# Two heads to a unit in the sparse-attention stage of a hybrid decoder layer

## The chip, the core and the metric

The kernel runs on one core of a Trainium2 chip. The metric is the device time of one execution in microseconds (us), median of the runs. The core's engines are TensorE (PE; its weight loads are shown as PEld), VectorE (DVE), ScalarE (ACT), GpSimd (POOL) and SyncE (SP), whose queue issues all transfers of this kernel.

## What is computed

One decoder layer on x of 1024 tokens by 1024 in float32: RMS norm, a projection of all branches, forgetting attention (FoX, 8 heads), native sparse attention (NSA, 8 heads that share 2 groups of keys and values), a gated merge, an output projection, an MLP with squared ReLU, a last norm. The change is in the NSA branch:

```python
# 8 heads of 64, 4 to a key/value group; query blocks of 128
p_cmp = masked_softmax(q @ kc.T * SCALE + bias_c, cmp_end <= qpos)      # 63 compressed keys
o_cmp = p_cmp @ vc
sel   = top_k(imp, 16)                # of 16 blocks of 64 keys: all of them
o_slc = masked_softmax(q @ k_slc.T * SCALE + bias, pos <= qpos) @ v_slc # causal
o_win = masked_softmax(q @ k_win.T * SCALE + bias, 0 <= qpos - pos < 512) @ v_win
o     = g0 * o_cmp + g1 * o_slc + g2 * o_win
merged = sigmoid(g_a) * (o_fox @ w_br_fox) + sigmoid(g_b) * (o @ w_br_nsa)
```

Float32 products are made of rounded high parts and remainders (`float32r`): a score takes two matmuls, a value product two (the rounded probabilities and their remainders against values stored as [high | low]), a projection three.

## The kernel before

`attention` runs two stages, FoX and NSA. In each, a list of units is worked off by `attend`. A unit of NSA (`nsa_unit`) is one head `h` and one pair `g` of query blocks, `a = 2g` and `b = 2g + 1`, so 32 units. It has two lists of steps:

- `s1`: for both query blocks the scores against compressed and selected keys, then against window keys (`scores`: two matmuls into a PSUM bank of tag `S`, then a VectorE instruction, L817, that adds the bias and finds the least value), and for each of three parts a `softmax` (exponential on ScalarE, reciprocal on VectorE, scaling by gate and sum on GpSimd).
- `s2`, made by `pv`: the probabilities go in chunks of up to four 128x128 blocks through TensorE transposes into a PSUM bank (`turn`, L160), ScalarE rounds them (L856), VectorE makes the remainders (L857), and two chunks later the value products add into `acc` (L157). When the last has been issued, `finish` adds the low rows to the high ones (L865, L866) and stores 64 x 256 results to `on_d`; those of the last head stay in SBUF.

`acc` is half of the one bank `accs`: `psA` gives the two halves in turn. A product has 256 columns, the two query blocks of one head. Three cases are not full: key block `b` is seen by query block `b` alone, and there the left half of the operand is a zero tile (`make_diag`; four matmuls of 256 columns a unit); the oldest window block `a - 4` is seen by query block `a` alone (two matmuls of 128 columns); the compressed part takes one matmul in place of two.

`attend` interleaves `s1` of a unit with `s2` of the one before (`interleave`, `s1` ahead by `LEAD`), and spreads a list `feed` of other TensorE work among them: projections of later heads and of the second key/value group, gates, the FoX half of the merge (`branch_fox`). `due` says which feed steps must have run before a unit, `holds` which may not run before one. Between the end of a unit's scores and its `s2` at least `LAT` (2 us by the planner's costs) of other work is set. The order of pairs within a head is `gorder = (3, 0, 2, 1)`, for head 4 `gorder4 = (0, 3, 2, 1)`. Row tiles exist twice for small pairs (g < 2) and twice for large ones. Bias rows `ww` (one tile a head, four transfers, two buffers) are loaded at a head's first unit; the bias of the compressed part, `wcmp`, is loaded for all heads at the start. At the end of the list `load_on` brings stored results back, `LEAVE` (7 us) of feed is kept for after the last unit, and `merge` begins with the NSA half of the merge, `branch(..., wide=True)`, 16 groups of twelve 512-column matmuls, each with two loads of `msn` tiles.

Of the kernel before, what the change touches and what calls it, by code (L numbers as in the profile page):

```python
# [124 lines left out]
class Kernel:  # L125
# [733 lines left out]
    def finish(self, pa, dst, j, q0, name):  # L859

        nc = self.nc
        own = slice(64 * j, 64 * j + 64)
        oth = slice(64 - 64 * j, 128 - 64 * j)
        t = self.att.tile([P, 256], F32, tag="ot", bufs=3, name=f"ot{name}")
        nc.scalar.copy(t[own], pa[oth])  # L865
        nc.vector.tensor_add(t[own], pa[own], t[own])  # L866
        if dst is not None:
            nc.sync.dma_start(dst[:, q0:q0 + 256], t[own])
            return
        on, c = self.on[q0 // H], slice(q0 % H, q0 % H + 256)  # L870
        nc.scalar.copy(on[own, 3, c], t[own])
        nc.vector.tensor_sub(on[own, 7, c], t[own], on[own, 3, c].bitcast(F32))
# [10 lines left out]
    def pv(self, chunks, acc_name, done):  # L883
# [14 lines left out]
        def mats(c):  # L898
            if state["first"]:
                box["acc"] = self.psA("acc" + acc_name)  # L900
            us = chunks[c][2](box[c])
            acc = box["acc"]
            for x, (w, th, tl, n) in enumerate(us):
                end = c == nch - 1 and x == len(us) - 1
                if tl is not None:
                    self.mm(acc[:, 0:n], w, tl, start=state["first"], stop=False)
                    state["first"] = False
                self.mm(acc[:, 0:n], w, th, start=False, stop=end)
            if c == nch - 1:
                done(acc)  # L910
# [9 lines left out]
    def fox_unit(self, h, g, qf, kf, vf):  # L920
# [45 lines left out]
        s2 = self.pv(chunks, f"f{h}_{g}", lambda acc: self.finish(acc, dst, j, g * 256, f"f{h}_{g}"))  # L966
# [12 lines left out]
    def nsa_unit(self, h, g, qf, ksf, kwf, vf):  # L979
        nc = self.nc  # L980
        j, g_ = h % 2, h // 4
        rows, s1 = {}, []

        def load_bias():
            if g == self.order(h)[0]:
                self.ww = self.att.tile([P, 640], F32, tag="ww", bufs=2, name=f"ww{h}")
                for x in range(4):
                    nc.sync.dma_start(self.ww[32 * x:32 * x + 32],
                                      ap(self.w_d, h * 32 * 768 + 127 - 32 * x, [[767, 32], [1, 640]]))
            rows["ww"] = self.ww  # L990

        s1.append((0, load_bias))
        a, b = 2 * g, 2 * g + 1
        for x, i in enumerate((a, b)):
            n = P * (i + 1)
            nm = f"n{h}_{i}"
            gt = lambda br, i=i: self.gate[:, i, 3 * h + br:3 * h + br + 1]
            t0 = max(0, i - 4)
            nw = P * (i + 1 - t0)

            def dp(x=x, nm=nm):
                if ("p", x) not in rows:
                    rows["p", x] = self.row_tile(g, "p" + nm)
                return rows["p", x]

            def dw(x=x, nm=nm):
                if ("w", x) not in rows:
                    rows["w", x] = (self.att.tile([P, CPAD + 512], F32, tag="W0", bufs=2, name="w" + nm) if g < 2
                                    else self.att.tile([P, CPAD + 640], F32, tag="W1", bufs=2, name="w" + nm))
                return rows["w", x]  # L1010

            near = max(0, n - 2 * P)
            spans = [(0, CPAD, "c", lambda i=i: self.wcmp[:, h, 56 - 8 * i:56 - 8 * i + CPAD],
                      lambda dw=dw: dw()[:, 0:CPAD])]
            if near:
                spans.append((CPAD, CPAD + near, "s",
                              lambda near=near: self.farb[:, h:h + 1].to_broadcast([P, near]), dp))
            spans.append((CPAD + near, CPAD + n, "s", lambda n=n, near=near: rows["ww"][:, 640 - (n - near):640],
                          lambda dp=dp, near=near: dp()[:, near:]))

            def slc_done(m, x=x, n=n, nm=nm, gt=gt):
                self.softmax(rows["w", x][:, 0:CPAD], m["c"], nm + "c", gt(0))
                self.softmax(rows["p", x][:, 0:n], m["s"], nm + "s", gt(1))

            self.scores(s1, qf, ksf, i, 0, spans, nm, slc_done)
            self.scores(s1, qf, kwf, i, t0 * P,
                        [(0, nw, "w", lambda nw=nw: rows["ww"][:, 640 - nw:640], lambda dw=dw: dw()[:, CPAD:])],
                        nm + "w",
                        lambda m, x=x, nw=nw, nm=nm, gt=gt: self.softmax(rows["w", x][:, CPAD:CPAD + nw], m["w"],
                                                                         nm + "w", gt(2)))  # L1030
        sb = lambda x, t: rows["p", x][:, t * P:(t + 1) * P]

        def wb(x, t):
            t0 = max(0, a + x - 4)
            return rows["w", x][:, CPAD + (t - t0) * P:CPAD + (t - t0 + 1) * P]

        cb = lambda x: rows["w", x][:, 0:P]
        vs = lambda t: vf()[:, t, 0, :]
        vw = lambda t: vf()[:, t, 1, :]
        pairs = [(lambda t=t: vs(t), lambda t=t: [sb(0, t), sb(1, t)]) for t in range(0, a + 1)]  # L1040
        pairs += [(lambda t=t: vw(t), lambda t=t: [wb(0, t), wb(1, t)]) for t in range(max(0, a - 3), a + 1)]
        pairs += [(lambda: self.vcmp[:, g_, :], lambda: [cb(0), cb(1)])]
        single = a >= 4
        chunks = []

        def pt(nb):
            th, tl = self.pt_tile(f"n{h}_{g}")
            return (th[:, 0:nb], tl[:, 0:nb]), th, tl

        def dg():  # L1050
            dh, dl = self.diag[self.dn % len(self.diag)]
            self.dn += 1
            dv = lambda t: t.rearrange("p (a b) -> p a b", b=P)[:, 1::2, :]
            return (dv(dh), dv(dl)), dh, dl

        x = 0
        while x < len(pairs) or single:
            two = pairs[x:x + 2]
            x += len(two)
            one = len(two) < 2 and single  # L1060
            if one:
                single = False
            nb = len(two) * 256 + (P if one else 0)
            fold = slice(256 * len(two) - 256, 256 * len(two)) if x == len(pairs) and two else None

            def blocks(two=two, one=one):
                r = [y for t in two for y in t[1]()]
                return r + ([wb(0, a - 4)] if one else [])

            def uses(bx, two=two, one=one, fold=fold):  # L1070
                r = []
                for y, t in enumerate(two):
                    c = slice(256 * y, 256 * y + 256)
                    r.append((t[0](), bx[1][:, c], None if c == fold else bx[2][:, c], 256))
                if one:
                    c = slice(256 * len(two), 256 * len(two) + P)
                    r.append((vw(a - 4), bx[1][:, c], bx[2][:, c], P))
                return r

            chunks.append((blocks, lambda nb=nb: pt(nb), uses, fold))  # L1080
# [4 lines left out]
        dst = self.on_d[h * HD:(h + 1) * HD, :] if h < NH - 1 else None  # L1085
        s2 = self.pv(chunks, f"n{h}_{g}", lambda acc: self.finish(acc, dst, j, g * 256, f"n{h}_{g}"))
        return s1, s2
# [3 lines left out]
    gorder4 = (0, 3, 2, 1)  # L1091

    def order(self, h):

        return self.gorder4 if h == 4 else self.gorder
# [3 lines left out]
    def attend(self, units, feed, holds=(), calls={}):  # L1099
# [7 lines left out]
        start = [0.0]  # L1107
        for u in units:
            start.append(start[-1] + sum(c for c, _ in u[0]) + sum(c for c, _ in u[1]))
# [26 lines left out]
        def one():  # L1136
            self.owed -= cum[self.fed + 1] - cum[self.fed]
            self.fed += 1
            while len(trail) > 1 and trail[1][0] <= self.att_ns - self.SLACK:
                trail.pop(0)  # L1140
# [6 lines left out]
        def emit(steps):  # L1147
            for c, f in steps:
                with self.tc.high_priority(offset=self.PRIO):
                    f()  # L1150
                self.att_ns += c
                if c:
                    trail.append((self.att_ns, self.last.ins))
                self.owed += c * rate()
# [18 lines left out]
    LAT1 = 8000.0  # L1173
    LEAD = 1.5
# [3 lines left out]
    def attention(self):  # L1178
# [71 lines left out]
        due, holds2 = [0] * 8 + [len(f2.steps)] * 8, []  # L1250
# [10 lines left out]
        for g in self.gorder4:  # L1261
            due.append(late[g > 1])
# [743 lines left out]
```

## Time and profile before

| | |
|---|---|
| median of 3 runs | 1605.89 us (1604.8 to 1607.16) |
| the profiled execution | 1607.07 us, its span 1605.3 us |
| TensorE busy | 1581.5 us of the span, 8333 matmuls and transposes |
| VectorE, ScalarE, GpSimd busy | 1091.5, 864.1, 349.9 us |

NSA units run from about 369 us to 857 us of the span. A matmul's recorded duration covers its whole passage, which overlaps the next one's; what one adds to a run of them is read from start to start.

### The profile page before, as it was taken

To read this page: it belongs to the slowest core of one execution; us is meant where nothing else is said; L and a number is where in the kernel's file an instruction comes from. 1 tells how busy PE (TensorE), PEld (TensorE's weight loads), DVE (VectorE), ACT (ScalarE), POOL (GpSimd) and SP (SyncE) were. 2 spreads that over 40 slices of the span, in tenths; PEclk is the share of its full clock that TensorE was granted. 3 is DMA by queue.
4 is the path that set the end of the run, shared out by engine and by line. 5 is a ranking of instruction groups with operands and counts; after the bars stand their busy time and mean duration, and the time that the engine had idled before them with its cause. 6 is when DMAs were issued, how large, how long until landed. Compare 5 with 4: busy or idle time off the path is not lost. (4 is left out here: it accounts for less than half of the span.)

```text
span 1605.3 us, 23955 instructions
## 1 busy us (share of the span) xinstructions
PE 1581.5 (99%) x8333; PEld 1345.2 (84%) x8333; DVE 1091.5 (68%) x2366; ACT 864.1 (54%) x1648; POOL 349.9 (22%) x431
## 2 busy tenths in 40 slices
PE   8999999999999999999999999999999999999997
PEld 7888888888888888898888888888888888888886
DVE  7656667656665675576766569766655689777876
ACT  6655656545554665567653256655555644333334
POOL 1122222122332322336430000233333100000004
PEclk9999999999999999999999999999999999999999
DMA  6311212342222212114338652554444696545312
GB/s 188 75 45 49 63 47 57 107 117 53 73 55 68 60 37 73 58 60 142 126 121 288 221 171 92 176 172 151 160 150 155 202 331 220 160 144 170 106 53 105
DMA packets 165233, 196.71 MB, mean 123 GB/s; under 512 B 21288, under 2 KB 100968, under 8 KB 165104
## 3 DMA queue, kind: packets, MB, share of 16 engines
q1 hardware_dynamic: 165112, 195.18, 38.3%
q8 instruction: 66, 1.08, 0.3%
q14 instruction: 55, 0.45, 0.1%
HBM read 139.99 MB, written 55.15 MB: 122 GB/s over the span
## 5 line engine op out<-in xcount | busy, mean ns | idle before, releaser
L157 PE MATMUL oX<-to,so 128*128 128x512 f32 x672 | 154.6, 389 | 0.0
L157 PEld LDWEIGHTS oX<-to,so 128*128 128x128 f32 x672 | 126.1, 188 | 26.2
L1836 ACT CAST to<-w 128x1024 fp32r<-128x1024 f32 x48 | 48.3, 1051 | 144.0 <-PE accs L157 53.2
L857 DVE TENSOR_TENSOR PTn<-ptn,PTn 128x512 fp32r<-128x512 f32 (+2 forms) x136 | 81.9, 610 | 49.0 <-ACT PTn L856 48.5
L856 ACT CAST PTn<-ptn 128x512 fp32r<-128x512 f32 (+2 forms) x136 | 69.4, 523 | 52.3 <-PE ptn L160 43.4
L157 PE MATMUL fX<-ht,w1h 128*128 128x512 f32 x384 | 95.0, 389 | 0.6 <-DVE ht L1542 0.6
L157 PE MATMUL accs<-PTn,Vnv 128*128 128x256 f32 x480 | 91.7, 305 | 0.0
L1674 POOL TENSOR_TENSOR ss<-w 128x512 f32<-128x512 f32 x14 | 22.1, 1580 | 314.2 <-DMA w<-in_w_ff_dram 193.6
L1947 POOL TENSOR_TENSOR z<-x,gf 128x512 f32<-128x512 f32 x14 | 18.7, 1354 | 308.0 <-DVE x L1885 303.8
L157 PEld LDWEIGHTS fX<-ht,w1h 128*128 128x128 f32 x384 | 72.0, 188 | 16.0 <-DVE ht L1542 1.1
L833 POOL TENSOR_SCALAR pf<-pf,rdf 128x896 f32<-128x896 f32 (+3 forms) x64 | 47.6, 749 | 164.9 <-DVE rdf L832 158.9
L157 PE MATMUL g<-hTl,wh_g 128*128 128x512 f32 (+1 forms) x288 | 77.9, 390 | 1.5 <-DVE hTl L308 1.5
L157 PE MATMUL oZ<-to,so 128*128 128x512 f32 x336 | 77.6, 389 | 0.0
L1664 DVE TENSOR_TENSOR w1l<-w,w1h 128x1024 fp32r<-128x1024 f32 (+1 forms) x32 | 34.6, 1081 | 60.0 <-ACT w1h L1663 60.0
L157 PEld LDWEIGHTS accs<-PTn,Vnv 128*128 128x128 f32 x480 | 72.6, 189 | 2.7 <-DVE otn L866 0.4
L157 PE MATMUL g<-hTh,wh_g 128*128 128x512 f32 (+1 forms) x288 | 74.5, 387 | 0.0
L157 PEld LDWEIGHTS oZ<-to,so 128*128 128x128 f32 x336 | 63.1, 188 | 13.1
L157 PE MATMUL g<-hTh,wl_g 128*128 128x512 f32 x256 | 72.0, 399 | 0.0
L1837 DVE TENSOR_TENSOR so<-hr,so 128x1024 fp32r<-128x1024 f32 x56 | 68.3, 1240 | 1.8 <-ACT so L1836 1.8
L1836 ACT CAST so<-hr 128x1024 fp32r<-128x1024 f32 x56 | 56.8, 1051 | 21.0 <-DMA hr<-hid_d 21.0
L830 ACT ACTIVATE pf<-pf,mf 128x896 f32<-128x896 f32 (+3 forms) x64 | 49.7, 777 | 24.3 <-DVE mf L817 21.6
L1837 DVE TENSOR_TENSOR to<-w,to 128x1024 fp32r<-128x1024 f32 x48 | 56.8, 1223 | 7.7 <-ACT to L1836 7.7
(521 smaller groups left out, 4322.0 us busy)
## 6 DMA issues: line engine op xcount, KB each, us to landing
w<-in_w_ff_dram SPq DMA_DIRECT2D x62, 512.0 KB, 4.7
hr<-hid_d SPq DMA_DIRECT2D x56, 512.0 KB, 4.6
wr_wo<-in_w_out_dram SPq DMA_DIRECT2D x20, 512.0 KB, 5.0
x<-in_x_dram SPq DMA_DIRECT2D x16, 512.0 KB, 6.8
wr_g<-in_w_in_dram SPq DMA_DIRECT2D x16, 512.0 KB, 3.9
hid_d<-h22s SPq DMA_DIRECT2D x32, 256.0 KB, 2.1
hid_d<-s2s SPq DMA_DIRECT2D x32, 256.0 KB, 2.0
hid_d<-s3h SPq DMA_DIRECT2D x32, 256.0 KB, 2.3
```

What stands on the lines that cost most here:

```text
L157: self.last = self.nc.tensor.matmul(*a, **k)
L830: nc.scalar.activation(p, p, AF.Exp, bias=nm, scale=-1.0, accum_out=den)
L833: nc.gpsimd.tensor_scalar(p, p, r, 1.0 if gate is None else gate, op0=OP.mult, op1=OP.mult)
L856: nc.scalar.copy(th, src)
L857: nc.vector.tensor_sub(tl, src, th.bitcast(F32))
L1664: nc.vector.tensor_sub(lo, src, hi.bitcast(F32))
L1674: e.tensor_add(p[:, 4:8], b[:, 0:4], b[:, 4:8])
L1836: nc.scalar.copy(o[:, 0, s], src)
L1837: nc.vector.tensor_sub(o[:, 1, s], src, o[:, 0, s].bitcast(F32))
L1947: nc.gpsimd.tensor_mul(y[:, c], x[:, c], gf[:, c])
```

## The change

A unit is now a pair `p` of heads that share keys and values, and a pair `g` of query blocks: 16 units. The probabilities of a key block for two heads and two query blocks stand side by side, and a value product has 512 columns into the whole of `accs`. Key block `b` is multiplied for query block `b` of both heads alone, into a strided half of `accs`, with no zero tiles; the window's oldest block the same way for query block `a`. The order within a pair is (0, 3, 1, 2). Row tiles exist once for each place of a unit, in two sets (small, large). `wcmp` is loaded at a pair's first unit (eight transfers), as is `ww` (eight; three buffers). `finish` adds two heads and stores 128 x 256. Only the last two units' results stay in SBUF. The feed holds one gate less ahead of the second value projection and three gates in halves; `load_on` is cut into steps; the NSA half of the merge goes through the first half of the tokens for six blocks of features, then the second half, then the last two blocks, with its place on TensorE fixed against the last attention steps. The DMA scratch of the program goes from the default to 256 bytes a partition.

```diff
-    def finish(self, pa, dst, j, q0, name):
+    def finish(self, pa, js, dst, q0, name):
...
+        for n, j in enumerate(js):
+            own = slice(64 * j, 64 * j + 64)
+            oth = slice(64 - 64 * j, 128 - 64 * j)
+            c = slice(256 * n, 256 * n + 256)
+            nc.scalar.copy(t[own], pa[oth, c])
+            nc.vector.tensor_add(t[own], pa[own, c], t[own])
...
-                box["acc"] = self.psA("acc" + acc_name)
+                box["acc"] = self.accs if whole else self.psA("acc" + acc_name)
...
+                o = n(acc) if callable(n) else acc[:, 0:n]
...
-    def nsa_unit(self, h, g, qf, ksf, kwf, vf):
+    def nsa_unit(self, p, g, qf, ksf, kwf, vf):
...
+            if g == self.order(p)[0]:
+                self.wc = self.att.tile([P, 2, 120], F32, tag="wcmp", bufs=2, name=f"wcmp{p}")
+                for x in range(8):
+                    nc.sync.dma_start(self.wc[16 * x:16 * x + 16],
+                                      ap(self.y_d, p * 4096 + 7 - x, [[128, 16], [2048, 2], [1, 120]]))
+                self.ww = []
+                for j in range(2):
+                    w = self.att.tile([P, 640], F32, tag="ww", bufs=3, name=f"ww{2 * p + j}")
...
+        of = lambda x: (lambda acc: acc.rearrange("p (j x q) -> p j x q", j=2, x=2)[:, :, x])
+        two = lambda t: t.rearrange("p (j q) -> p j q", j=2)
...
-        chunks.append((lambda: [sb(1, b), wb(1, b)], dg,
-                       lambda bx: [(vs(b), bx[1][:, 0:256], bx[2][:, 0:256], 256),
-                                   (vw(b), bx[1][:, 256:512], bx[2][:, 256:512], 256)]))
+        for t in range(a + 1):
+            chunks.append((lambda t=t: [sb(j, x, t) for j, x in four], lambda: pt(H),
+                           lambda bx, t=t: [(vs(t), bx[1], bx[2], H)]))
+        for t in range(max(0, a - 3), a + 1):
+            chunks.append((lambda t=t: [wb(j, x, t) for j, x in four], lambda: pt(H),
+                           lambda bx, t=t: [(vw(t), bx[1], bx[2], H)]))
+        chunks.append((lambda: [cb(j, x) for j, x in four], lambda: pt(H),
+                       lambda bx: [(self.vcmp[:, g_, :], bx[1], None, H)], slice(0, H)))
+        if a >= 4:
+            chunks.append((lambda: [wb(j, 0, a - 4) for j in range(2)], lambda: pt(256),
+                           lambda bx: [(vw(a - 4), two(bx[1][:, 0:256]), two(bx[2][:, 0:256]), of(0))]))
+        chunks.append((lambda: [sb(0, 1, b), sb(1, 1, b), wb(0, 1, b), wb(1, 1, b)], lambda: pt(H),
+                       lambda bx: [(vs(b), two(bx[1][:, 0:256]), two(bx[2][:, 0:256]), of(1)),
+                                   (vw(b), two(bx[1][:, 256:H]), two(bx[2][:, 256:H]), of(1))]))
...
+    KEEP = (3, 1), (3, 2)
...
-    gorder4 = (0, 3, 2, 1)
+    norder = (0, 3, 1, 2)
...
-            self.make_diag(np_, 1, (0, 2))
...
+            order = [(f, half) for fs in (range(6), range(6, 8)) for half in (0, 1) for f in fs]
...
+                with (self.tc.issue_after(self.ends[-4 if x < 4 else -1]) if wide and x > 1 else nullcontext()):
+                    part_(i, f, fx, half, n, box, x)
...
-    nc = _bacc.Bacc("TRN2", target_bir_lowering=False, num_devices=1)
+    nc = _bacc.Bacc("TRN2", target_bir_lowering=False, num_devices=1, dynamic_dma_scratch_size=256)
```

## Rows read from the trace of the kernel before

**Rows 1.** The page: span, then busy us (share) and instructions.
```profile
span 1605.3 us, 23955 instructions
PE 1581.5 (99%) x8333; PEld 1345.2 (84%) x8333; DVE 1091.5 (68%) x2366; ACT 864.1 (54%) x1648; POOL 349.9 (22%) x431
```

**Rows 2.** Windows of the NSA stage: stretch, length, each engine's busy us, clock, DMA.
```profile
390.00:482.00 92.00, 92.00 (x542) 81.24 (x541) 55.55 (x204) 53.10 (x131) 28.91 (x46) 1.00 0.23 63
482.00:543.00 61.00, 61.00 (x358) 53.63 (x357) 35.05 (x135) 33.78 (x87) 19.62 (x32) 1.00 0.23 64
600.00:660.00 60.00, 59.08 (x333) 51.18 (x331) 32.48 (x91) 31.67 (x72) 15.05 (x24) 1.00 0.24 71
724.00:775.00 51.00, 49.60 (x306) 43.47 (x305) 35.65 (x136) 37.73 (x94) 33.55 (x40) 1.00 0.44 144
857.00:866.00 9.00, 7.78 (x35) 6.12 (x34) 2.74 (x6) 1.05 (x1) 0.00 (x0) 1.00 0.83 267
```

**Rows 3.** Waits of PE from 390 to 866: us in total, times, longest.
```profile
PE ptn L160 <- DVE PTn L857: 1.9, 2, 1.1
PE sn_4w L157 <- DVE mn L817: 1.6, 1, 1.6
PE brn L157 <- DVE msn L1435: 1.2, 1, 1.2
PE ptn L160 <- DVE rdn_1s L832: 0.6, 1, 0.6
```

**Rows 4.** Groups by form, PE, whole span: count, busy us, mean ns.
```profile
L157 PE MATMUL accs<-PTn,Vnv 128*128 128x256 f32 x448 | 86.6, 309 | 0.0
...
L160 PE MATMUL ptn<-idn,wn 128*128 128x128 f32 x304 | 59.8, 272 | 0.0
L160 PE MATMUL ptn<-idn,pn 128*128 128x128 f32 x288 | 52.4, 274 | 2.5 <-DVE PTn L857 1.9 <-DVE rdn_1s L832 0.6
...
L157 PE MATMUL accs<-diag,Vnv 128*128 128x256 f32 x128 | 20.9, 285 | 0.0
...
L157 PE MATMUL accs<-PTn,vcmp 128*128 128x256 f32 x32 | 9.4, 294 | 0.0
...
L157 PE MATMUL accs<-PTn,Vnv 128*128 128x128 f32 x32 | 5.4, 249 | 0.0
```

**Rows 5.** Timeline of PE, three places: start us, us, instructions.
```profile
403.98 0.34 PE L157 MATMUL accs<-PTn,Vnv 128*128 128x128 f32 x2
404.15 0.41 PE L160 MATMUL ptn<-idn,pn 128*128 128x128 f32 x2
...
413.86 0.64 PE L157 MATMUL accs<-PTn,Vnv 128*128 128x256 f32 x4
414.34 0.39 PE L157 MATMUL g<-hTl,wh_g 128*128 128x512 f32 x1
...
599.98 1.99 PE L157 MATMUL nk<-hTh,wl_nk 128*128 128x512 f32 x8
601.80 0.39 PE L157 MATMUL nk<-hTl,wh_nk 128*128 128x512 f32 x1
```

**Rows 6.** Groups by form, DVE, 385 to 862 us: count, busy us, mean ns.
```profile
L857 DVE TENSOR_TENSOR PTn<-ptn,PTn 128x512 fp32r<-128x512 f32 x104 | 70.9, 689 | 45.7 <-ACT PTn L856 45.4
```

**Rows 7.** The page's DMA queues: packets, MB, share.
```profile
q1 hardware_dynamic: 165112, 195.18, 38.3%
q8 instruction: 66, 1.08, 0.3%
q14 instruction: 55, 0.45, 0.1%
```

**Rows 8.** Tile `accs`, 745 to 750 us: ns min/median/max, first and last start.
```profile
L157 PE MATMUL accs<-diag,Vnv x4: 277/282/384, 745.5 to 746.0; 128*128 128x256 f32 x4
...
L157 PE MATMUL accs<-PTn,Vnv x4: 281/282/386, 749.1 to 749.5; 128*128 128x256 f32 x4
L865 ACT COPY otn<-accs x1: 365/365/365, 748.2 to 748.2; 64x256 f32<-64x256 f32 x1
L866 DVE TENSOR_TENSOR otn<-accs,otn x1: 427/427/427, 748.6 to 748.6; 64x256 f32<-64x256 f32 x1
...
  PEld accs L157: 0.4, 1
```

**Rows 9.** Timeline of SP: start us, us, transfers issued.
```profile
351.14 3.59 SPq L988 DMA_DIRECT2D ww<-w_d  x8
354.77 3.87 SPq L1320 DMA_DIRECT2D wcmp<-y_d  x8
...
420.03 1.72 SPq L988 DMA_DIRECT2D ww<-w_d  x4
```

**Rows 10.** DMA issues: count, KB each, median us to landing.
```profile
ww<-w_d SPq DMA_DIRECT2D x32, 80.0 KB, 2.0
```

**Rows 11.** Timelines of PE and DVE: a first score, the last result.
```profile
369.44 1.02 PE L157 MATMUL sn<-ks,Qnq 128*128 128x512 f32 x4
...
856.62 0.42 DVE L872 TENSOR_TENSOR on<-otn,on 64x256 fp32r<-64x256 f32 x1 [0.47 <-ACT on L871]
```

More of the change, by code (lines that the diff above doesn't have):

```diff
@@ L881, in row_tile, with pv @@
         return self.att.tile([P, T], F32, tag="P1", bufs=2, name=name)
-    def pv(self, chunks, acc_name, done):
+    def pv(self, chunks, acc_name, done, whole=False):
         nc = self.nc
@@ L977, in make_diag @@
             self.diag.append((t[:, 0], t[:, 1]))
-    def nsa_unit(self, h, g, qf, ksf, kwf, vf):
+    def nsa_unit(self, p, g, qf, ksf, kwf, vf):
         nc = self.nc
-        j, g_ = h % 2, h // 4
+        g_ = p // 2
         rows, s1 = {}, []
+        a, b = 2 * g, 2 * g + 1
         def load_bias():
[L985 to L990, printed above, removed]
-        s1.append((0, load_bias))
[L993 to L1033, printed above, removed]
@@ L1056, in nsa_unit @@
[L1056 to L1080, printed above, removed]
@@ L1087, in nsa_unit, with order @@
+        dst = None if (p, g) in self.KEEP else self.on_d[p * P:(p + 1) * P, :]
+        s2 = self.pv(chunks, f"n{p}_{g}", lambda acc: self.finish(acc, (0, 1), dst, g * 256, f"n{p}_{g}"), True)
         return s1, s2
+    KEEP = (3, 1), (3, 2)
     gorder = (3, 0, 2, 1)
-    gorder4 = (0, 3, 2, 1)
-    def order(self, h):
-        return self.gorder4 if h == 4 else self.gorder
+    norder = (0, 3, 1, 2)
+    def order(self, p):
+        return self.norder
     LAT = 2000.0
@@ L1107, in attend @@
         start = [0.0]
+        wt = [(id(e), self.WS) for u in units for e in u[0]] + [(id(e), self.WV) for u in units for e in u[1]]
+        wt = dict(wt)
         for u in units:
-            start.append(start[-1] + sum(c for c, _ in u[0]) + sum(c for c, _ in u[1]))
+            start.append(start[-1] + self.WS * sum(c for c, _ in u[0]) + self.WV * sum(c for c, _ in u[1]))
         marks = [(start[v], u[2]) for v, u in enumerate(units)] + [(start[-1], len(feed))]
@@ L1138, in one @@
             self.fed += 1
+            if self.STATIC:
+                with self.tc.issue_after(self.last.ins):
+                    feed[self.fed - 1][1]()
+                return
             while len(trail) > 1 and trail[1][0] <= self.att_ns - self.SLACK:
@@ L1147, in emit @@
         def emit(steps):
-            for c, f in steps:
-                with self.tc.high_priority(offset=self.PRIO):
+            for e in steps:
+                c, f = e
+                with self.tc.high_priority(offset=self.PRIO), (
+                        self.tc.issue_after(self.last.ins) if self.STATIC else nullcontext()):
                     f()
+                c *= wt[id(e)]
                 self.att_ns += c
@@ L1153, in emit @@
                     trail.append((self.att_ns, self.last.ins))
+                    self.ends = self.ends[-3:] + [self.last.ins]
                 self.owed += c * rate()
@@ L1173 @@
     LAT1 = 8000.0
+    ends = []
+    STATIC = False
+    WS, WV = 1.0, 1.0
     LEAD = 1.5
@@ L1340 @@
     LEAVE = 7000.0
-    ON2 = 24
-    ON3 = 31
+    ON = 9, 17, 25
+    ON3 = 16
     FST = 6
@@ new lines, in branch, with part, part_ @@
+        ns = [self.wadd([(None, wa[:, f2 * 256:f2 * 256 + 256].rearrange("(k p) c -> p k c", p=P))],
+                        f"br{name}{f2}", shape=(4, 256)) for f2 in range(4)]
+        order = [(f, half) for f in range(8) for half in range(2)]
+        if wide:
+            order = [(f, half) for fs in (range(6), range(6, 8)) for half in (0, 1) for f in fs]
+        for x, (f, half) in enumerate(order):
+            n, fx, box = ns[f // 2], f % 2, {}
+            def part(i, f=f, fx=fx, half=half, n=n, box=box, x=x):
+                with (self.tc.issue_after(self.ends[-4 if x < 4 else -1]) if wide and x > 1 else nullcontext()):
+                    part_(i, f, fx, half, n, box, x)
+            def part_(i, f, fx, half, n, box, x):
+                hi, lo = self.wget(n)
+                if i == 0:
+                    box["sg"] = stage(f, half)
+                    psf = self.psS if wide and x % 5 > 1 else self.psP
+                    box["ps"] = psf(f"br{name}{f}{half}")
+                o = of()[half]
+                mm = [(w, k + d) for ks in ((0, 1, 2), (3,)) for w, d in ((lo, 0), (hi, 4), (hi, 0))
+                      for k in ks]
+                for m in range(6 * i, 6 * i + 6):
+                    w, k = mm[m]
+                    self.mm(box["ps"], w[:, k % 4, fx * P:(fx + 1) * P], o[:, k],
+                                     start=m == 0, stop=m == 11)
+                if i == 1:
+                    done(f, half, box["ps"], box["sg"])
+            for i in range(2):
+                st.add(6 * MM, lambda i=i, part=part: part(i), n)
```

165 lines of the change are left out of this document (85 added, 80 removed).

## The prediction

> **What bounds the kernel now.** I read the page's engine line first: TensorE is busy 1581.5 us of a span of 1605.3 us, the next engine, VectorE, 68% [rows 1]. A busy matmul row need not mean TensorE at its peak, so the second view is the windows of the NSA stage, read for stretches that fall short: from 390 to 543 us TensorE is busy without a gap and at the full granted clock of 1.00 (2.4 GHz), later stretches lack 0.9 to 1.4 us each, while VectorE stands at about 60% [rows 2]. The third view, TensorE's waits from 390 to 866 us, gives the size of everything that is not TensorE work: 1.9 + 1.6 + 1.2 + 0.6 = 5.3 us in five waits [rows 3]. So the stage lasts as long as TensorE's own list of instructions takes from start to start. A change is worth what it takes off that list, less or plus what it does to 5.3 us of waits. Work saved on other engines counts for nothing directly.
>
> **Value products: what is removed.** The counts before are 448 products of 256 columns on key blocks, 128 on the half-zero operands, 32 on the compressed part, and 32 of 128 columns on the oldest window block [rows 4]. After, by the diff: two heads share a product, so 448 + 32 become 240 of 512 columns; a unit's four products on block `b` serve two heads, so 128 become 64 of 256 columns; the 32 of 128 become 16 of 256. That is 640 matmuls before, 320 after.
>
> The recorded mean of about 300 ns is the whole passage of one matmul and no price. The price is start to start: four products of 256 columns from 413.86 to 414.34 us are 0.120 us each (0.1175 to 0.1225 with the rounding of both ends); eight matmuls of 512 columns from 599.98 to 601.80 us are 0.2275 us each; two of 128 columns take 0.17 us together [rows 5]. I take the low reading of the 256-column price, since a small gap could stand in the place read:
>
> - before: 608 x 0.1175 + 16 x 0.17 = 71.4 + 2.7 = 74.1 us
> - after: 240 x 0.2275 + 80 x 0.1175 = 54.6 + 9.4 = 64.0 us
> - difference: 10.1 us.
>
> Bounds: at 0.120 us it is 75.7 - 64.2 = 11.5 us. If only columns counted, at the 512-column rate of 0.2275/512 = 0.444 ns a column, 159,744 columns become 143,360, and 7.3 us are saved. Of the 10.1 us, the dropped zero columns (64 x 0.1175) make 7.5, the rest is the fixed few nanoseconds of 320 matmuls.
>
> These two prices can be weighed against the Trainium skill ("TensorE: Matmul & The Clock Gate", section "Back-to-back issue gap"), which gives an isolated full-clock gap of N/2.4 + 2.5 ns, 109 ns at 256 columns and 216 ns at 512. Both rows here are 5 to 10% above it; by the page's prices the saving would be an estimated 7.7 us, near my lower bound.
>
> **What stays.** Scores keep their pieces and number. The transposes stay 304 + 288 [rows 4], since every block of probabilities is still turned once. By the code, chunks fall from 184 to 152, so ScalarE and VectorE evict fewer, fuller banks; a full remainder on VectorE takes 689 ns [rows 6], and neither engine sets the end of this stage [rows 2]. That goes at nothing, hidden behind TensorE; if the cover were gone it would still be a gain. The zero tile's four GpSimd instructions go, at nothing. The smaller DMA scratch touches no transfer of this kernel as far as the queues show: all packets but 121 instruction fetches are on the hardware queue [rows 7]; cost nothing, its room goes to the larger row tiles. Moving a gate and splitting one more in halves leaves the same matmuls.
>
> **What is added: one accumulator.** The first product of a unit now waits until `finish` of the unit before has read the whole bank. In the trace that wait already shows: at one boundary the last product starts at 746.0 us, ScalarE's copy comes late at 748.2, VectorE's sum ends at 749.0, and the next unit's first product starts at 749.1, after a wait of 0.4 us on the weight load [rows 8]. Two heads add one sum of about 0.43 us behind the first, the second copy running beside it. TensorE normally has two groups of transposes and scores to do before it needs the bank. Floor: no wait, 0. Ceiling: every one of 15 boundaries as late as this one with the second sum on top, 15 x 0.83 = 12.5 us. I take 0.6 us: near the floor, since TensorE's waits in the whole stage name `finish` nowhere [rows 3].
>
> **What is added: loads at a pair's start.** Eight loads of `wcmp` and eight of `ww` per pair, where a head had four. Issue costs 0.43 to 0.48 us each (8 in 3.59, 8 in 3.87 us), landing 2.0 us [rows 9, 10], so 7.5 us of SP's queue and about 9.5 us until the last has landed. Most of it can be issued as early as now: the loads for head 2 go out at 420.03 us [rows 9], long before that head. Only the second head's `ww` must wait, with three buffers, until the first head of the running pair has had its last scores, half a unit's scores ahead. From the first score at 369 us to the last result at 857 us [rows 11] a pair unit lasts (857 - 369)/16 = 30 us on average, so that half is some 8 to 13 us ahead, and four loads need 4 x 0.45 + 2.0 = 3.8 us. Behind a waiting load on SP stand weight loads of the feed, which run two tiles ahead, and stores that nobody awaits. Cost nothing from below (no gain is possible), 9.5 us at each of three pair starts from above; I take nothing.
>
> **What is moved.** The order small, large, small, large keeps two units of one size from following each other; before, head 4's order set 1 next to 0 and 3 next to 2, and the wait of 1.6 us on the scores of block 4 lies there. Against it, the second group's keys must still be written between units 7 and 8, so that wait may return. Waits at unit starts (`ptn` on PTn and on `rdn_1s`, 2.5 us [rows 3]) can come 16 times instead of 32, each with twice the product work of the unit before to cover it: I take 1.2 us off. The merge's wait of 1.2 us comes from the loads of `msn`, whose room is freed by the end of the stage; this end is later relative to the loads (a large unit is last), and half the loads lie ahead as before: left as it is, bounds 0 and 3 us.
>
> **Sum.** -10.1 + 0.6 - 1.2 = -10.7 us. The profiled execution took 1607.07 us, its span 1605.3; the median of the runs is 1605.89. So the changed span should be about 1594.6, and the median 1605.9 - 10.7 = 1595.2 us.
>
> **Rivals.**
>
> - *Columns only, waits as before.* The saving is 7.3 us and the waits come to the same 5.3 us or up to 2 us more: 1598.6 to 1600.6 us. For it: transposes stand between products over most of the stage, so the fixed cost of a product may be hidden in part.
> - *Waits vanish too.* 11.5 us and all 5.3 us of waits: 1589.1 us. Against it: the merge's loads and the keys of the second group remain.
> - *The bank is the bound.* A wait at each boundary, 5 to 12.5 us in all: 1600 to 1607 us. Against it: a single 0.4 us in 31 boundaries as shown.
> - *Strided outputs.* The 80 products on single query blocks write two runs of 128 columns apart. No row before has such an output. If one cost twice its price, 80 x 0.1175 = 9.4 us return and the time is 1604.6 us, no change. The Trainium skill ("PSUM — Partial Sum Buffer", section "Specifications (TRN2)") says that any non-contiguous access pattern slows matmuls significantly; no run here shows it.
> - *Slower: pair loads come late.* If the waiting `ww` load holds SP's queue, then VectorE's first bias sums of the second head, and soon TensorE with three score banks full, stand for up to 9.5 us at three pair starts: 1595.2 + 28.5 = 1623.7 us. It decides from 3.6 us a pair on (10.7/3), and is slower than before beyond the measurement from 4.7 us. Against it: the lead of 8 to 13 us.
>
> **How the numbers follow.** Chances: the forecast, 1592 to 1598 us, 0.57; columns only 0.15; waits vanish 0.08; the bank 0.09; strided outputs 0.05; pair loads 0.06. The forecast and the first two rivals hold 0.80, so the range reaches from 1589 to 1602 us, which also takes in the mild half of the bank's case. About 0.2% (3.2 us) is what a measurement of this kernel can tell from no change: the first three cases and half of the bank's are faster, strided outputs and the rest of the bank's the same, late loads slower: 0.86, 0.08, 0.06.
>
> **What would show it.** TensorE's count falls by 320 to 8013 and its busy time by about 10 us; the runs of 512-column value products read 0.2275 us from start to start, those with strided outputs 0.12; the NSA stage ends some 10 us earlier and everything behind it keeps its length; TensorE's waits in the stage stay at 3 to 6 us. Wrong would be: a wait of `accs` weight loads on `otn` at most boundaries, a wait of `sn` scores on L817 behind `ww` at three places about a fourth of the stage apart, a strided product of 0.2 us or more, or a gap of several us where the merge begins.

## The result, and the profile after

The changed kernel takes 1591.7 us (median of 4 runs, 1591.63 to 1591.98), the kernel before 1605.78 us (4 runs, 1604.8 to 1607.16). The ratio is 0.9912, with an interval of 0.9895 to 0.9929: 14.1 us less, where 10.7 were forecast. The direction and the range held; the size is off by 3.4 us, and even the mild end of the interval (0.0071 x 1605.8 = 11.4 us) lies above the forecast. The time is just outside the band of 1592 to 1598 us that the forecast gave itself, and nearer to the rival in which the waits vanish too (1589.1 us) than to the forecast's 1595.2. The same kernel was run twice more, on two chips, each time beside the kernel before: 1592.21 and 1591.68 us, ratios 0.9909 and 0.9908. So the miss is no accident of one run.

The page after: span, then busy us, share and instructions of each engine, and the queue that carries the data.

```profile
span 1590.0 us, 23189 instructions
PE 1569.0 (99%) x8013; PEld 1320.0 (83%) x8013; DVE 1087.5 (68%) x2316; ACT 856.8 (54%) x1598; POOL 348.5 (22%) x427
...
q1 hardware_dynamic: 165400, 195.18, 38.3%
```

TensorE has 320 instructions less, as counted ahead, and 12.5 us less busy time, where about 10 were expected; it is still the only engine near its span; its queue of data carries the same 195.18 MB as before [rows 1, 7]. Where the 15.3 us of span went is read from three marks: the first `nq` matmul (the NSA stage's start), the first `wo` matmul (the merge's end) and the end. TensorE's timeline after, at the first two (start us, us, instructions):

```profile
337.70 2.11 PE L157 MATMUL nq<-hTh,wl_nq 128*128 128x512 f32 x8
...
873.84 0.62 PE L157 MATMUL wo<-wh_wo,ml 128*128 128x512 f32 x2
```

and before:

```profile
338.10 1.65 PE L157 MATMUL nq<-hTh,wl_nq 128*128 128x512 f32 x6
...
888.63 0.61 PE L157 MATMUL wo<-wh_wo,ml 128*128 128x512 f32 x2
```

Between the marks lie 550.5 us before and 536.1 after: 14.4 us of the 15.3. Ahead of them 0.4 us are gone and behind them 0.5 (716.7 to 716.2), where nothing was changed. How much such a stretch moves by itself is seen from the other runs of equal kernels below: 549.5 us for the kernel before with nothing but the smaller scratch, 536.4 and 536.4 for the two repeats of the changed one. So the stage gave 13.1 to 14.4 us.

TensorE's waits from 380 to 862 us of the changed kernel (us in total, times, longest):

```profile
PE accs L157 <- DVE PTn L847: 1.2, 2, 0.7
PE accs L157 <- DVE PTn L857: 1.0, 2, 0.5
```

These two lines answer to [rows 3]. 5.3 us in five waits became 2.2 us in four. None of the old places is left: not the scores of block 4 behind L817, not the first transposes behind L857 or L832, not the merge behind `msn`. What is left is of another kind: a value product (`accs`) waits for VectorE's eviction of its chunk. In the two waits for L847 it is the compressed chunk near the end of a unit's list; of the two for L857 one stands at a unit's first product (751.85 us), one among the window chunks of the last unit (831.56 us). And no line names `otn`: no wait for the single accumulator shows.

The groups by form on TensorE (count, busy us, mean ns, idle before):

```profile
L157 PE MATMUL accs<-PTn,Vnv 128*128 128x512 f32 x224 | 79.0, 433 | 1.0 <-DVE PTn L857 1.0
...
L160 PE MATMUL ptn<-idn,wn 128*128 128x128 f32 x304 | 51.9, 272 | 0.0
...
L160 PE MATMUL ptn<-idn,pn 128*128 128x128 f32 x288 | 48.1, 272 | 0.0
...
L157 PE MATMUL accs<-PTn,Vnv 128*128 128x256 f32 x80 | 13.5, 283 | 0.0
...
L157 PE MATMUL accs<-PTn,vcmp 128*128 128x512 f32 x16 | 7.0, 439 | 1.2 <-DVE PTn L847 1.2
```

240 products of 512 columns and 80 of 256, and as many transposes as in [rows 4]. Their prices stand in the timeline, start to start:

```profile
790.64 1.09 PE L157 MATMUL accs<-PTn,Vnv 128*128 128x512 f32 x4
791.57 0.60 PE L160 MATMUL ptn<-idn,wn 128*128 128x128 f32 x4
...
840.70 0.64 PE L157 MATMUL accs<-PTn,Vnv 128*128 128x256 f32 x4
841.17 0.86 PE L157 MATMUL brn<-on,wl_brn 128*128 128x512 f32 x3
```

Four products of 512 columns take 0.93 us, 0.2325 us each (0.2275 was forecast). Four of 256 columns with strided outputs take 0.47 us, 0.1175 us each: the price of plain ones [rows 5]. Over all of them the median spacing is 0.236 us for 512 columns and 0.118 us for 256, and 0.120 us for the 448 plain ones before.

A product beside a transpose takes longer to the next start than one beside a product, and the transpose behind it less, so the two are added up: all products and transposes of the stage, from each start to the next, without the idle time before an instruction. By the records of the traces this is 88.6 + 45.1 = 133.7 us before and 75.0 + 48.6 = 123.6 us after, 10.1 us less. The kernel before with the smaller scratch gives 133.7, the two repeats 123.6 each.

### The profile page after: what moved, and what is told of

Its sections match the earlier page's. It is cut to its first block, busy times and chain, and to the rows that moved or that the text cites. A ratio compares the mean times of both kernels' runs of the same rounds, so it can differ in the third digit from the quotient of the medians.

```text
span 1590.0 us, 23189 instructions
## 1 busy us (share of the span) xinstructions
PE 1569.0 (99%) x8013; PEld 1320.0 (83%) x8013; DVE 1087.5 (68%) x2316; ACT 856.8 (54%) x1598; POOL 348.5 (22%) x427
## 3 DMA queue, kind: packets, MB, share of 16 engines
q1 hardware_dynamic: 165400, 195.18, 38.3%
## 5 line engine op out<-in xcount | busy, mean ns | idle before, releaser
L857 DVE TENSOR_TENSOR PTn<-ptn,PTn 128x512 fp32r<-128x512 f32 (+1 forms) x136 | 91.2, 672 | 64.9 <-ACT PTn L856 63.9
L856 ACT CAST PTn<-ptn 128x512 fp32r<-128x512 f32 (+1 forms) x136 | 76.6, 570 | 72.2 <-PE ptn L160 61.1
L157 PE MATMUL accs<-PTn,Vnv 128*128 128x512 f32 (+1 forms) x304 | 92.6, 393 | 1.0 <-DVE PTn L857 1.0
L157 PEld LDWEIGHTS oZ<-to,so 128*128 128x128 f32 x336 | 63.1, 188 | 13.1
L830 ACT ACTIVATE pn<-pn,mn 128x128 f32<-128x128 f32 (+3 forms) x64 | 49.6, 776 | 18.6 <-DVE mn L817 16.3
```

The lines of the kernel that those rows point to most:

```text
L157: self.last = self.nc.tensor.matmul(*a, **k)
L830: nc.scalar.activation(p, p, AF.Exp, bias=nm, scale=-1.0, accum_out=den)
L856: nc.scalar.copy(th, src)
L857: nc.vector.tensor_sub(tl, src, th.bitcast(F32))
```

## The experiments

The stretch "stage" is always from the first `nq` to the first `wo` matmul of the run's profiled execution; 536.1 to 536.4 us for the changed kernel, with a mean of 536.3 in its three profiles, and 2.2 to 2.5 us of waits, with a mean of 2.4.

### The zero columns put back

The unit's last chunk multiplies key block `b` for the other query block too, by a tile of zeros: 64 more products of 256 columns. This has the columns of the kernel before (143,360 + 64 x 256 = 159,744) in 256 fewer matmuls.

```diff
-                       lambda bx: [(vs(b), two(bx[1][:, 0:256]), two(bx[2][:, 0:256]), of(1)),
-                                   (vw(b), two(bx[1][:, 256:H]), two(bx[2][:, 256:H]), of(1))]))
+                       lambda bx: [(x, y, z, of(q)) for x, c in ((vs(b), 0), (vw(b), 256)) for y, z, q in
+                                   ((two(bx[1][:, c:c + 256]), two(bx[2][:, c:c + 256]), 1),
+                                    (two(self.zz), two(self.zz), 0))]))
...
+            self.zz = np_.tile([P, 256], FR, tag="zz", bufs=1, name="zz")
...
```

> The changed kernel with the zero columns back: each unit also multiplies block b against a zero tile for query block a, 64 more products of 256 columns (strided output); the result is the same. Theory (the stage lasts as long as TensorE's list): 64 x 0.1175 = 7.5 us more, 1599.2 us. Rival (the stage is by now paced by waits on ScalarE and VectorE, and the work saved was only part of it): less than 3 us more, 1592 to 1594.5 us.

Measured: 1599.54 us, ratio 0.9961 (0.9949 to 0.9974), span 1597.6. The stage took 543.7 us (337.8 to 881.5), 7.4 more than the changed kernel's; 64 x 0.1175 = 7.5 were forecast. The waits of TensorE in its stage:

```profile
PE accs L157 <- DVE PTn L857: 1.0, 2, 0.6
PE accs L157 <- DVE PTn L847: 0.7, 1, 0.7
PE brf L157 <- DVE msf L1417: 0.3, 1, 0.3
```

2.0 us, as little as in the changed kernel, so the zero columns cost their full price. This run also parts the rest, though less sharply: with the same columns as before, the stage is 5.8 to 6.8 us shorter (549.5 and 550.5 against 543.7). 2.4 to 3.3 us of this are waits (4.4 and 5.3 against 2.0), and 3.4 to 3.5 us are left. If all of that came from the 256 fewer matmuls, it would be 13 ns for each. But products and transposes, summed as above, take 132.15 us here against 133.7, 1.6 us less or 6 ns for each; the gates' matmuls, whose number no edit touched, read 156.7 us against 158.5 in the same sum. So fewer matmuls at the same columns gave something between 1.6 and 3.5 us, and where the rest belongs stays open.

### The order, the merge's place, FoX

The order within a pair starts with a large unit and ends with a small one:

```diff
-    norder = (0, 3, 1, 2)
+    norder = (3, 0, 2, 1)
```

> The changed kernel with the pairs in the order (3, 0, 2, 1), large units first and small last, still large and small in turn. Theory (product work made the gain, order is worth the waits only): TensorE's waits in the stage grow from 2.2 to at most 5 us, 1592 to 1595 us. Rival (the order and the end of the stage made the third of the gain that the product sum did not hold): 3.6 us or more, 1595.3 us or above.

Measured: 1596.98 us, 0.9942 (0.993 to 0.9955), span 1595.3; the stage 541.3 us, 5.0 more. TensorE's waits in it:

```profile
PE accs L157 <- DVE PTn L857: 1.5, 2, 1.3
PE ptn L160 <- DVE PTn L857: 1.4, 2, 0.8
PE ptn L160 <- POOL pn L833: 0.9, 1, 0.9
PE sn_4w L157 <- DVE mn_1w L817: 0.5, 1, 0.5
PE accs L157 <- DVE PTn L847: 0.5, 1, 0.5
```

4.8 us, as the theory had it at most, but the time is the rival's: 5.3 us above the changed kernel's. The waits are 2.4 us more than there, and transposes wait again. The other 2.6 us are in no line of this view. Gaps of less than 0.15 us, which it leaves out, are 0.45 us more. And each stop costs more than its gap: a matmul with no successor behind it is recorded to the end of its passage (0.40 us for a 512-column product), where with one behind it the next starts after 0.236 us. There are 16 stops here, short ones counted, against 6; by the median spacing of each form this comes to an estimated 2.6 against 1.1 us; the trace models the ends of matmuls, so it is no more than an estimate. The last 0.7 us stay open.

The merge goes through its blocks as before, without a fixed place:

```diff
-            order = [(f, half) for fs in (range(6), range(6, 8)) for half in (0, 1) for f in fs]
+            pass
...
-                with (self.tc.issue_after(self.ends[-4 if x < 4 else -1]) if wide and x > 1 else nullcontext()):
+                with (self.tc.issue_after(self.ends[-4 if x < 4 else -1]) if False else nullcontext()):
```

> The changed kernel with the NSA half of the merge in the old order (both halves of the tokens for each block of features, no place fixed against the last attention steps). Theory (the forecast left this step as it is, 0): the wait at the start of the merge comes back as before, 1.2 us, 1592.9 us. Rival (nothing: the wait vanished because the loads come earlier for other reasons): 1591.7 us within 0.5 us. A third way: with a large unit last the loads come later than before, 3 us or more.

Measured: 1595.62 us, 0.9935 (0.9922 to 0.9947), span 1593.9; the stage 539.9 us, 3.6 more. The timeline of TensorE where the stage's last unit ends (in brackets the idle time before, and what ended it):

```profile
845.87 0.74 PE L157 MATMUL accs<-PTn,Vnv 128*128 128x256 f32 x4 [1.17 <-DVE PTn L857]
848.81 1.62 PE L157 MATMUL brn<-on,wl_brn 128*128 128x512 f32 x4 [2.21 <-ACT on L874]
850.23 3.17 PE L157 MATMUL brn<-on,wh_brn 128*128 128x512 f32 x8
853.24 0.84 PE L157 MATMUL brn<-on,wl_brn 128*128 128x512 f32 x3
```

and its windows (stretch, length, busy us of PE, PEld, DVE, ACT, POOL, granted clock, DMA):

```profile
843.00:849.00 6.00, 2.63 (x16) 2.00 (x15) 2.50 (x6) 1.72 (x4) 0.00 (x0) 1.00 0.01 3
849.00:853.00 4.00, 4.00 (x11) 3.16 (x11) 2.58 (x5) 0.82 (x1) 0.00 (x0) 0.57 0.66 174
853.00:858.00 5.00, 5.00 (x24) 4.13 (x22) 4.78 (x8) 1.37 (x3) 0.00 (x0) 1.00 0.89 301
```

After the last product everything stands until two heads have been added and cast: 2.21 us. Then the clock granted is 0.57, most of 4 us at the lower level of 1.2 GHz, and the 12 matmuls from 848.81 to 853.24 us take 0.369 us each instead of 0.2275: 1.7 us more. Waits (4.5 against 2.2 to 2.5) and clock together make 3.7 to 4.0 us, against 3.6 measured. The third way's size came, but not by its cause: the wait is for the last result `on`, not for loads. The same place of the changed kernel, TensorE:

```profile
840.70 0.64 PE L157 MATMUL accs<-PTn,Vnv 128*128 128x256 f32 x4
841.17 0.86 PE L157 MATMUL brn<-on,wl_brn 128*128 128x512 f32 x3
841.87 1.53 PE L157 MATMUL brn<-on,wh_brn 128*128 128x512 f32 x6
```

and ScalarE and VectorE beside it:

```profile
842.22 0.36 ACT L867 COPY otn<-accs 64x256 f32<-64x256 f32 x1 [0.48 <-DVE otn L868]
843.08 0.41 ACT L874 CAST on<-otn 128x256 fp32r<-128x256 f32 x1 [0.49 <-DVE otn L868]
...
843.52 0.43 DVE L875 TENSOR_TENSOR on<-otn,on 128x256 fp32r<-128x256 f32 x1 [0.47 <-ACT on L874]
```

The last product is at 841.17 us over and the result is there only at 843.95, but TensorE goes on without a gap, with blocks of the merge for the first half of the tokens, which the fixed place kept back for this stretch.

Another run takes the zero tiles out of FoX's value products too: 64 products of 256 columns become 128 columns wide.

```diff
...
-        chunks.append((lambda: [blk(1, a + 1), blk(0, a), blk(1, a)], dg,
-                       lambda b: [(v(a + 1), b[1][:, 0:256], b[2][:, 0:256], 256),
-                                  (v(a), b[1][:, 256:512], b[2][:, 256:512], 256)]))
...
+        chunks.append((lambda: [blk(0, a), blk(1, a), blk(1, a + 1)], pt3,
+                       lambda b: [(v(a), b[1][:, 0:256], b[2][:, 0:256], 256),
+                                  (v(a + 1), b[1][:, 256:384], b[2][:, 256:384], lambda acc: acc[:, P:256])]))
...
```

> The changed kernel with no zero tiles in the FoX stage either: 64 products of 256 columns, of which half were zeros, become 128 columns. By the 0.17 us that two products of 128 columns take in the trace before: 64 x (0.1175 - 0.085) = 2.1 us less, 1589.6 us. If only columns count: 64 x 0.057 = 3.6 us less, 1588.1 us. If a matmul of 128 columns costs as much as a transpose, 0.11 us: 0.5 us less, 1591.2 us.

Measured: 1590.65 us, 0.9903 (0.9888 to 0.9918), span 1588.8. The first `nq` matmul starts at 336.6 us instead of 337.7: 1.1 us for 64 products, 17 ns each, between the 2.1 us of the first case and the 0.5 of the last. The products themselves came nearer to the first: in the trace a product of 128 columns takes 0.087 us to the next start on average (about 0.06 or 0.11 by its neighbour), as the 0.17 us for two had said, and FoX's products and transposes together take 1.6 us less than in the changed kernel (64.65 against 66.25). The start of the stage alone moves by a few tenths between runs of equal kernels (337.6 to 337.9 us), so the stretch can't tell the price of one product.

### The order and the scratch alone, in the kernel before

```diff
-    gorder4 = (0, 3, 2, 1)
+    gorder4 = (0, 3, 1, 2)
...
-        return self.gorder4 if h == 4 else self.gorder
+        return self.gorder4
```

> The kernel before with the order (0, 3, 1, 2) for every head and nothing else changed. Undoing this order in the changed kernel cost about 4.5 us of waits. If the order is worth that by itself, in units of one head too: 4 to 5 us below the kernel before, about 1601.5 us. If it is worth only the wait between head 3 and head 4 (two units of one size in a row): 1 to 2 us below, 1604.5 us. If the order pays only together with units of two heads: within 0.5 us of before.

Measured, over 11 runs: 1607.91 us, 1.0009 (1.0 to 1.0018), span 1605.5. The order by itself is worth nothing: the median is even 1.9 us above the kernel before, outside all three cases. (The 4.5 us of waits that the text above speaks of were 4.8 in all, of which 2.4 were added.) Its waits in the stage (380 to 866 us) come to 5.9 us and changed their places:

```profile
PE brf L157 <- DVE msf L1398: 1.5, 1, 1.5
PE accs L157 <- DVE PTn L857: 1.5, 2, 0.9
PE brn L157 <- ACT on L871: 1.3, 1, 1.3
PE ptn L160 <- DVE PTn L857: 0.9, 1, 0.9
PE accs L157 <- DVE otn L866: 0.7, 1, 0.7
```

Two of these lines bear on the changed kernel. With a large unit last the merge waits for the last result `on` here too, 1.3 us for one head where the run above lost 2.2 us for two. And the accumulator is waited for once (`otn`, 0.7 us), though this kernel has two halves of it.

The 256-byte scratch alone (one argument in the program's constructor):

> The kernel before with the DMA scratch of 256 bytes alone. Theory (no transfer of this kernel uses it): the same time as before within 0.5 us. Rival (part of the gain comes from it): 2 us or more below.

Measured, over 11 runs: 1606.32 us, 0.9998 (0.9989 to 1.0007). Nothing. As it is the kernel before in all else, its profile is a second reading of that. Of the waits of [rows 3] the first, second and fourth come again with the same 1.9, 1.6 and 0.6 us; the merge's was 1.2 us there and is less here:

```profile
PE brn L157 <- DVE msn L1435: 0.3, 1, 0.3
```

### The changed kernel again, and a try at its last wait

The changed kernel once more, beside a version that has FoX's edit and takes the compressed chunk second in a unit's list instead of near its end, so that the product that waits for L847 would have its operand early:

```diff
-        chunks.append((lambda: [cb(j, x) for j, x in four], lambda: pt(H),
-                       lambda bx: [(self.vcmp[:, g_, :], bx[1], None, H)], slice(0, H)))
+        chunks.insert(1, (lambda: [cb(j, x) for j, x in four], lambda: pt(H),
+                          lambda bx: [(self.vcmp[:, g_, :], bx[1], None, H)], slice(0, H)))
```

> The changed kernel unchanged, on the same chip as the others of this call, so that small differences can be read: 13.5 to 15 us below the kernel before; its TensorE waits in the NSA stage about 2.2 us.

> The changed kernel with no zero tiles in FoX and the compressed chunk second in a unit's list in place of last but one or two, so that its single short product no longer stands where little other work is left to cover its eviction. Theory (the two waits of TensorE on L847, 1.2 us, go away and nothing takes their place): 1.2 us below the FoX variant, about 3 us below the changed kernel. Rival (the wait moves to the last chunk's eviction, L857): no more than 0.3 us below the FoX variant.

Measured: 1592.21 us, 0.9909 (0.9896 to 0.9923), and 1592.0 us, 0.9909 (0.9896 to 0.9923). The changed kernel is 13.8 us below the kernel before, as expected, with 2.5 us of waits. The other brings no gain; against FoX's edit alone its stage is 1.3 to 1.7 us longer (537.7 against 536.0 and 536.4). The view of waits says why:

```profile
PE accs L157 <- DVE PTn L857: 2.9, 4, 1.2
PE sn L157 <- DVE mn L817: 0.2, 1, 0.2
```

The waits for L847 are gone, and those for L857 have grown from 1.0 to 2.9 us: taking one chunk's wait away only moved it to others, as the rival had it.

### Two large units in a row, and two repeats

```diff
-    norder = (0, 3, 1, 2)
+    norder = (0, 3, 2, 1)
```

> The changed kernel with the pairs in the order (0, 3, 2, 1): within a pair of heads two large units follow each other, and at the seam two small ones. If units of one size in a row are what costs (their row tiles exist once, so the second unit's exponentials wait until the first is transposed): waits at four places of 1.5 us or more, 6 us or more above the changed kernel. If only the ends of the stage matter (first unit, last unit): as the changed kernel, within 1.5 us.

Measured: 1620.41 us, 1.0086 (1.0071 to 1.0101), span 1617.2: 28.7 us slower than the changed kernel beside it, and slower than the kernel before: the theory's way, but far beyond its 6 us, with 26 waits in the view instead of four. The stage took 563.5 us, 27.2 more. The four largest waits in it, and one window:

```profile
PE ptn L160 <- DVE PTn L857: 6.2, 10, 2.1
PE accs L157 <- DVE PTn L857: 3.9, 6, 1.3
PE sn L157 <- DVE mn L817: 1.5, 3, 0.7
PE sn_7w L157 <- DVE mn L817: 1.1, 1, 1.1
...
760.00:800.00 40.00, 34.48 (x175) 27.88 (x175) 24.96 (x85) 18.86 (x42) 9.40 (x13) 0.96 0.24 79
```

In the timeline a stretch of this window shows what the two units lack:

```profile
774.62 0.50 PE L157 MATMUL accs<-PTn,Vnv 128*128 128x512 f32 x1 [0.50 <-DVE PTn L857]
774.95 0.27 PE L160 MATMUL ptn<-idn,pn 128*128 128x128 f32 x1
774.98 0.48 PE L157 MATMUL accs<-PTn,Vnv 128*128 128x512 f32 x1
775.29 0.49 PE L160 MATMUL ptn<-idn,pn 128*128 128x128 f32 x3
```

From 767.7 to 783.2 us TensorE has transposes and value products only, and stands for an eviction of L857 before 769.4, 772.0, 774.6, 777.2 and 779.8 us, 0.49 to 1.29 us each time. By the code the row tiles exist once for each place of a size, so the next large unit's scores can't be written until this one has been transposed, and the scores that stand between transposes elsewhere are not there. That the missing second set of row tiles is the cause is read from the code and this stretch; no run gave the large units one.

All waits of the view come to 14.6 us, 12.2 more than in the changed kernel. The granted clock is 0.96 from 760 to 800 us and 0.97 from 800 to 860 us; taken as time at the lower of its two levels, this is an estimated 3.4 us. Of what is left, an estimated 6 us is again the passage of the matmul ahead of a stop: there are 44 stops against 6. Some 5 us stay open.

The two repeats:

> The changed kernel without zero tiles in FoX either, again, beside the changed kernel on one chip. From the FoX stretch of its trace (1.1 us shorter): 1.0 to 1.3 us below the changed kernel, with intervals that do not touch. If the earlier gap came from the chip: within 0.4 us.

> The changed kernel, for the two above: 13.5 to 15 us below the kernel before.

Measured: 1591.0 us, 0.9905 (0.9888 to 0.9921), for FoX's edit on top, and 1591.68 us, 0.9908 (0.9894 to 0.9923), for the changed kernel. FoX's part was 0.8 us shorter (first `nq` at 336.8 against 337.6 us). It is the fastest version seen, twice, but only 0.7 us below the changed kernel beside it, less than the 1.0 to 1.3 us expected and less than the intervals separate.

## Why the prediction was right, and where its sizes failed

**What bounds the kernel: right.** The time is TensorE's list: the stage's 7.4 us for 64 products put back, with 2.0 us of waits, show it best, and the zero columns' 7.5 us were the largest part of the forecast's sum.

**Value products: right, in size too.** The step came to 10.1 us with the lower reading of the 256-column price, 0.1175 us, and to 11.5 with 0.120. Products and transposes together became 10.1 us shorter in the traces (133.7 to 123.6). Some luck is in how near that is: 512 columns were priced at 0.2275 us, read from projections, where four value products took 0.2325 each, and 240 x 0.005 = 1.2 us less would have been saved by that price alone. The rival "columns only" had 7.3 us here and 1598.6 to 1600.6 us in all; both are refuted. The estimate of 7.7 us by the prices of the Trainium skill ("TensorE: Matmul & The Clock Gate", section "Back-to-back issue gap") is too low as well: its 109 and 216 ns lie below the 0.1175 and 0.2325 us read here. How much of a matmul's price is fixed, the runs leave open: the medians of 0.120 and 0.236 us give 2 x 0.120 - 0.236 = 4 ns, the zero-column run 6 ns in the products and transposes and 13 ns if the whole stage is charged to them.

**What is moved: the step that failed in size.** It left the merge as it was, took 1.2 us off the waits at unit starts, and let the keys' wait return: with the accumulator's 0.6 us, 4.7 us of waits were to remain, and 3 to 6 us were named as what would show the forecast. 2.2 remained (2.5 and 2.4 in the repeats). The stage became 14.4 us shorter with 3.1 us fewer waits, and 13.2 us shorter against the scratch run (549.5 to the mean of three, 536.3) with 2.0 us fewer (4.4 to a mean of 2.4), where the forecast had 0.6 us fewer. So 1.4 to 2.5 us of the miss of 3.4 are waits. The rival in which they vanish too, given 0.08, was nearer to what happened to them, though not all are gone and it priced the products at 11.5 us. Another 1.1 to 1.2 us, for which the forecast has no term, lie in the stage's matmuls other than products and transposes: the 672 of the gates alone read 158.5 us before and 157.5 after. Their steps were moved and cut by the change, but no run did that alone, so its cause stays open. In parts: the waits at unit starts (2.5 us) and the keys' wait (1.6 us) vanished, not by half but wholly, and 2.2 us at products that wait for an eviction took their place; the merge's wait is gone, though it was 1.2 us in the kernel before and 0.3 with the smaller scratch.

Two things that the step counted as free turned out to be needed. Without the merge's new order and place the larger last unit has nothing to cover its two sums, and the old one would have cost 3.6 us, 1.7 of them through the clock. And the order within a pair is no preference but a condition: large units back to back cost 28.7 us, twice what the change gives, and large ahead of small 5.0 us in the stage. That the same order alone gave 1.0009 in the kernel before shows that it earns nothing of itself; it only fits the larger tiles.

**One accumulator: the floor was right.** 0.6 us was taken; no wait on `otn` is shown in any of the three profiles of the changed kernel. The bank's rival is refuted: it needed a wait at each boundary, and none shows at any.

**Strided outputs: refuted.** 0.1175 us each, the price of plain ones. The rule of the Trainium skill ("PSUM — Partial Sum Buffer", section "Specifications (TRN2)") that non-contiguous access slows matmuls significantly does not show here, for two runs of 128 fp32 columns.

**Pair loads: refuted.** TensorE's waits name L817 nowhere. SP's timeline and VectorE's first bias sum with `ww` of the second pair show the lead:

```profile
449.70 1.71 SPq L1000 DMA_DIRECT2D ww<-w_d  x4
...
464.35 0.29 DVE L817 CUSTOM_DVE_ANT_0 pn<-sn,ww 128x128 f32<-128x128 f32 x1
```

These held-back loads go out 14.6 us before their pair begins, those of the other two pairs 19.1 and 14.8 us, and they need under 4; 8 to 13 us ahead of the second head's scores alone had been estimated.

**Scratch: right at nothing**, by a run of its own. **Evictions: not quite nothing.** They were put down as hidden behind TensorE; with VectorE at 68% and ScalarE at 54% most are, but all 2.2 us of waits that are left are for evictions of L847 and L857.

**A slip in the chances.** The first three cases and half of the bank's add up to 0.845, and strided outputs with the other half to 0.095, where 0.86 and 0.08 were stated.

**Open.** About 0.7 us of what the order (3, 0, 2, 1) costs, and some 5 us of what (0, 3, 2, 1) costs, have no place. Products of 512 columns cut into two of 256, without any other edit, were not tried, and neither were the feed's changes by themselves.

## What to carry to other kernels

Where one engine's list is the time, count its instructions and columns and price them start to start, with prices taken from the stage itself, products and the transposes between them together; putting the removed work back, alone, checks that price in one run. Larger units halve the places where a wait can arise, but each needs its cover: ask which other matmuls stand between a unit's transposes and behind its last product, for both were worth more here than any wait in the profile before. A reordering that measures as nothing by itself can still be what a larger change stands on.

## What the runs showed of the hardware

A short stop cost more than its length, in two ways. After a stretch with TensorE busy 2.63 of 6 us the granted clock was 0.57 over the next 4 us, and 1.7 us were lost on top of the 2.21 us of the last wait. And where the clock held, a 512-column product with nothing behind it was recorded at 0.40 us, where the next one otherwise starts after 0.236: with the order (3, 0, 2, 1) 16 stops cost an estimated 2.6 us beyond their gaps. A value product of 512 columns took 0.2325 us, one of 256 took 0.1175, with its output in two strided runs as well, and one of 128 took 0.087 on average; narrowing 64 products from 256 to 128 columns brought their stretch forward by only 0.8 to 1.1 us. And one wait, the merge's for its loads, moved from 1.2 to 0.3 us between two executions that differ only in the DMA scratch, while the other four kept theirs: a single wait for a load is poor ground for a term of a sum.
